# A two-layer mLSTM, attention and RG-LRU backbone: the attention's second projection group as steps between the attention units

## The chip, the cores and the metric

The kernel runs on one core of a Trainium2 chip, in one launch. The metric is the device time of the launch in microseconds; a figure for a kernel is the median of several runs.

## What is computed

Two layers work on 1024 latent tokens (a grid of 16 rows and 64 columns) and 256 context tokens of width 1024, all in f32. Of each layer the part in question is the neighbourhood attention of 8 heads of 64: projections q, k, v from the normed input, an RMS norm of q and k, scores against a window of 8 x 16 grid places with a relative bias and against all 256 context tokens, softmax, and the weighted sum of v.

```python
def row_block(r):
    sr = jnp.clip(r - wr // 2, 0, rows - wr)
    q_r = lax.dynamic_index_in_dim(qg, r, axis=1, keepdims=False)
    k_band = lax.dynamic_slice_in_dim(kg, sr, wr, axis=1)
    ...
    s_loc = jnp.einsum('bqhd,brqchd->bhqrc', q_r, k_win).astype(jnp.float32) * scale
    dr = sr + jnp.arange(wr) - r + (WIN_R_MAX - 1)
    bias = jnp.transpose(rpb[:, dr][:, :, dc], (0, 2, 1, 3))
    s_loc = (s_loc + bias.astype(jnp.float32)).reshape(b_, NA_HEADS, GRID_W, wr * wc)
    s_ctx = jnp.einsum('bqhd,bkhd->bhqk', q_r, kc).astype(jnp.float32) * scale
    p = jax.nn.softmax(jnp.concatenate([s_loc, s_ctx], axis=-1), axis=-1).astype(v.dtype)
```

Beside it in each layer run an mLSTM of 4 heads, an RG-LRU, the output projection over all three, and an MLP of hidden width 4096. Context tokens attend to context alone, and have no output in the second layer.

## The kernel before

**Split matmuls.** Every f32 weight and activation is split into a rounded high part and a low rest (`wh`, `wl` by `load_w`; `xh`, `xlo`), and each product takes three matmuls: high-high, high-low, low-high. An input projection of one token tile (128 tokens, 256 columns) is 24 matmuls into one PSUM bank (`proj_tm`).

**PSUM.** Eight banks: one `p`, one `q`, three `a`, two `b`, one `c`. `bank("pq")` takes turns between p and q.

**Stages of a layer.** RG-LRU and mLSTM projections; the mLSTM's state and output (`ml_state`, `ml_out`); then attention. The eight heads are two groups of four, and each group two pairs. `na_group(grp)` projects k, q and v of a group (10 token tiles each in layer 0; q only 8 in layer 1), ScalarE copies each result (`uev`), squares it for the norm (`usq`), and the copy goes to DRAM (`u_nk`, `u_nq`, `u_nv`). Group 0 stands in the program right behind `ml_out`, group 1 behind group 0.

**Preparation.** `na_prep(hp)` makes the stacks of a pair of heads: it loads `ut`, multiplies by the norm, transposes on TensorE, and writes split keys and queries (`KH`, `KL`, `QS`), of which one partition half is filled by DMAs from the other half. There are two sets of stacks, for even and for odd pairs. Pair 0 is prepared before attention begins; pair hp + 1 is prepared in six (layer 1: five) parts beside the units of pair hp.

**Attention units.** `na_att(hp)` has 10 units a pair in layer 0 (two of context queries, eight of latent ones) and 8 in layer 1, so 40 and 32. A unit computes scores into the three `a` banks (L834, L838; context L780), VectorE adds the table and takes the maximum (L848, L852), ScalarE takes the exponential, `side()` issues other work, and `softmax_pv` transposes (L727), scales and multiplies by v (L757).

**Tables.** The relative bias of a head is expanded by DMAs on GpSimd's queue from `R_d` to `E_d` to `T_d` in DRAM (`tab_expand`, `tab_rows`). Each pair loads three sets of two tables (`tab`, four buffers), and GpSimd adds to each a combined mask (`crm`, rows and columns, six made per program).

**The filler.** `side()` also issues `fill()`, the first half of the output projection (L1363, bank p, evacuated by VectorE at L1380 with `xs`), 24 steps over 40 units in layer 0, 16 over 32 in layer 1.

**Modulation.** In layer 0, `mod_pairs` loads 32 blocks of `w_mod` in 16 pairs (`mr`, two buffers) and multiplies them (L316), one pair at every third projection step of both groups.

**Order.** The program is recorded in the order of the code, and a list scheduler with a time model then arranges each engine's instructions. So the order of the code sets priorities; what stands in each engine's queue is what the scheduler made of it. Nearly all DMAs go through SP's queue, in order.

## Time and profile before

| what | before |
|---|---|
| median of 3 runs | 3124.81 us (3122.93 to 3128.83) |
| profiled execution | 3124.27 us, span 3122.5 us |
| TensorE busy | 3020.2 us, 97% |
| VectorE busy | 1900.0 us, 61% |
| ScalarE busy | 1128.4 us, 36% |
| GpSimd busy | 291.0 us, 9% |
| mean granted TensorE clock | 0.988 |
| attention, layer 0 | about 510 to 755 us |
| attention, layer 1 | about 2125 to 2347 us |

TensorE's busy share counts a matmul from issue to end, and matmuls overlap, so "busy" is not "at its peak". The granted clock of a stretch is the mean over its time at two levels, 1.2 and 2.4 GHz: 1.00 is all at 2.4. The attention stages are found by their first scores and last products with v.

### The profile page before, as it was taken

The numbers are of one execution on the slowest core, as the hardware profiler recorded it, in microseconds if no ns is written. First come the engines' busy times: TensorE is split into PE (matmuls) and PEld (weight loads), VectorE is DVE, ScalarE is ACT, GpSimd is POOL, SyncE is SP. The second block draws the span as 40 slices with busy tenths as digits, with TensorE's granted clock in tenths as the row PEclk, the third lists the DMA queues.
The fourth block names the chain that finished last, engine by engine and source line by source line (L and its number), as shares of the span: only waits on it lengthen the run. The fifth ranks groups of instructions, "written<-read, shape, count | busy, mean of one in ns | idle before, by whom it ended". The sixth has DMA issues, their size and how long they took to land.

```text
span 3122.5 us, 47474 instructions
## 1 busy us (share of the span) xinstructions
PE 3020.2 (97%) x18250; PEld 2558.1 (82%) x18250; DVE 1900.0 (61%) x4318; ACT 1128.4 (36%) x2011; POOL 291.0 (9%) x252
## 2 busy tenths in 40 slices
PE   7999998999899999999999999998899999999999
PEld 6888898778788888887778889997787777887877
DVE  5757655787977667455444574765787444444444
ACT  4632223574421222233222453234564222332222
POOL 0410000222200000010000511002222000000000
PEclk8999999999999999999999999999999999999999
DMA  9624567765233444233323632347753332333233
GB/s 272 216 73 144 171 190 199 226 169 178 68 115 105 126 124 125 75 108 101 95 88 94 175 123 82 100 131 219 219 172 110 95 95 89 99 116 91 92 96 93
DMA packets 531098, 410.73 MB, mean 132 GB/s; under 512 B 27580, under 2 KB 496536, under 8 KB 530872
## 3 DMA queue, kind: packets, MB, share of 16 engines
q1 hardware_dynamic: 519448, 387.41, 41.9%
q0 software_dynamic: 8576, 15.00, 1.5%
q10 hardware_dynamic: 2848, 5.28, 0.5%
q8 instruction: 144, 2.36, 0.3%
q14 instruction: 82, 0.67, 0.1%
HBM read 339.72 MB, written 67.53 MB: 130 GB/s over the span
## 4 chain that ended last, share of the span: by engine, by line
PE 70%; DVE 11%; DMA 10%; issue 2%; ACT 2%; SPq 1%; POOL 0%; ACTq 0%; DVEq 0%; POOLq 0%
PE psa L468 14%; PE psa L1515 13%; PE psq L468 5%; PE psp L468 5%; PE psp L1515 4%; DMA mr<-in_w_mod_dram 4%; PE psq L1515 4%; PE psp L483 4%; PE psq L483 3%; PE psp L1363 3%; DVE ma L344 3%; PE psc L757 2%; PE psb L727 1%; PE psa L1363 1%; PE psa L834 1%
## 5 line engine op out<-in xcount | busy, mean ns | idle before, releaser
L200 ACT ACTIVATE wh<-wr 128x1024 fp32r<-128x1024 f32 (+3 forms) x356 | 361.8, 1021 | 929.7 <-PE psa L1515 296.3
L201 DVE TENSOR_TENSOR wl<-wr,wh 128x1024 fp32r<-128x1024 f32 (+3 forms) x356 | 424.5, 1196 | 380.6 <-ACT wh L200 374.3
L468 PE MATMUL psa<-xlo,wh 128*128 128x512 f32 (+1 forms) x856 | 319.5, 373 | 2.2 <-DVE xlo L444 2.1
L468 PE MATMUL psa<-xh,wh 128*128 128x512 f32 (+1 forms) x856 | 318.8, 373 | 2.4 <-ACT xh L443 2.4
L468 PE MATMUL psa<-xh,wl 128*128 128x512 f32 (+1 forms) x856 | 319.3, 373 | 1.4 <-DVE wl L201 1.4
L1515 PE MATMUL psa<-hl,wh 128*128 128x512 f32 (+1 forms) x768 | 286.1, 373 | 1.3 <-DVE hl L211 1.3
L1515 PE MATMUL psa<-hh,wh 128*128 128x512 f32 (+1 forms) x768 | 284.6, 376 | 0.6 <-ACT wh L200 0.5
L1515 PE MATMUL psa<-hh,wl 128*128 128x512 f32 (+1 forms) x768 | 278.1, 373 | 0.6 <-DVE wl L201 0.6
L1519 DVE SCALAR_TENSOR_TENSOR res<-psa,modt,res 128x512 f32<-128x512 f32 (+1 forms) x192 | 130.9, 693 | 165.8 <-PE psa L1515 165.6
L468 PEld LDWEIGHTS psa<-xlo,wh 128*128 128x128 f32 x856 | 161.6, 189 | 33.4 <-DVE xlo L444 2.9
L468 PEld LDWEIGHTS psa<-xh,wh 128*128 128x128 f32 x856 | 161.5, 189 | 33.4 <-ACT xh L443 2.8
L468 PEld LDWEIGHTS psa<-xh,wl 128*128 128x128 f32 x856 | 161.6, 189 | 32.5 <-DVE wl L201 2.2
L409 POOL TENSOR_TENSOR acc<-acc,nsq 128x512 f32<-128x512 f32 (+1 forms) x56 | 80.3, 1446 | 1020.6 <-ACT nsq L408 970.7
L210 ACT ACTIVATE hh<-rl 128x512 fp32r<-128x512 f32 (+1 forms) x160 | 93.5, 589 | 225.0 <-DVE rl L1491 225.0
L1515 PEld LDWEIGHTS psa<-hh,wh 128*128 128x128 f32 x768 | 144.5, 188 | 34.8 <-ACT wh L200 8.9
L483 PE MATMUL psp<-wl,xh 128*128 128x256 f32 (+1 forms) x560 | 163.1, 291 | 5.9 <-DVE wl L201 5.8
L1515 PEld LDWEIGHTS psa<-hh,wl 128*128 128x128 f32 x768 | 144.5, 188 | 28.6 <-DVE wl L201 1.5
L1515 PEld LDWEIGHTS psa<-hl,wh 128*128 128x128 f32 x768 | 144.6, 188 | 27.8 <-DVE hl L211 1.5
L483 PE MATMUL psp<-wh,xh 128*128 128x256 f32 (+1 forms) x560 | 162.2, 290 | 2.5 <-ACT wh L200 2.4
L483 PE MATMUL psq<-wh,xh 128*128 128x256 f32 (+1 forms) x560 | 162.7, 290 | 1.4 <-ACT usq L641 0.8
L483 PE MATMUL psq<-wl,xh 128*128 128x256 f32 (+1 forms) x560 | 160.9, 287 | 0.0
L483 PE MATMUL psq<-wh,xlo 128*128 128x256 f32 (+1 forms) x560 | 160.2, 286 | 0.0
(409 smaller groups left out, 7342.4 us busy)
## 6 DMA issues: line engine op xcount, KB each, us to landing
wr<-in_w_mlp_dram SPq DMA_DIRECT2D x256, 512.0 KB
mr<-in_w_mod_dram SPq DMA_DIRECT2D x92, 512.0 KB
wr<-in_w_in_dram SPq DMA_DIRECT2D x48, 512.0 KB
tab<-T_d SPq DMA_DIRECT2D x48, 384.0 KB
T_d<-E_d POOLq DMA_DIRECT2D x48, 256.0 KB, 6.5
ab<-row_d SPq DMA_DIRECT2D x36, 256.0 KB
xT_d<-res SPq DMA_DIRECT2D x4, 2048.0 KB
wr<-in_w_out_dram SPq DMA_DIRECT2D x32, 256.0 KB
```

Of the source, the lines that this page charges most:

```text
L200: act.activation(hi[:, a:b], raw[:, a:b], AF.Copy)
L201: dve.tensor_sub(lo[:, a:b], raw[:, a:b], hi[:, a:b].bitcast(F32))
L210: act.activation(hi, src32, AF.Copy)
L344: dve.scalar_tensor_tensor(a, raw[:, k], s[:, k], a, op0=OP.mult, op1=OP.add)
L409: pool.tensor_add(acc[bi], acc[bi], sq[:, :n])
L468: m = pe.matmul(t[:, :n], w[a][:, k, :], X[bi][b][:, k, :], start=(i == 0), stop=(i == 23))
L483: m = pe.matmul(t[:, :cols], X[bi][b][:, half * 4 + k, o:o + P], ws[half][a][:, k, :], start=(i == 0), stop=(i == 23))
L727: pe.transpose(t[:w, j * P:(j + 1) * P], S[e][:, o:o + w], permT)
L757: pe.matmul(to[64 * e:64 * e + 64, :P], vals[i][:w, 64 * e:64 * e + 64], PT[:w, e, i], start=(i == 0), stop=(i == nt - 1))
L1363: pe.matmul(t[:, :n], w[a][:, k, cc * P:(cc + 1) * P], Y[bi][b][:, k], start=(i == 0), stop=(i == 11))
L1515: m = pe.matmul(t[:, :n], w[a][:, k, cc * P:(cc + 1) * P], H[bi, k][b], start=(i == 0), stop=(i == 3 * GH - 1))
L1519: dve.scalar_tensor_tensor(xr[bi][:, ct], t[:, :n], G2[:, ct, v:v + 1], xr[bi][:, ct], op0=OP.mult, op1=OP.add)
```

## The change

- **Group 1's projections become steps.** `proj_tm` yields after each token tile. `proj = na_group(1, "p")` uses bank p alone. Five steps stand beside the preparation of pair 0 and five beside that of pair 1; the other 20 (layer 1: 18) are spread over the first 15 (12) attention units. The norms of q and k come before v.
- **The filler is moved behind them.** The output projection's first half now spreads over the remaining 25 (20) units, and its pools are opened when the last projection step is done.
- **One set of stacks.** Pairs 0, 1 and 3 write the same buffers, pair 2 others. Pair 1 is prepared after pair 0's units, no longer beside them; pairs 2 and 3 still beside units.
- **Column masks in the bias.** `tab_mask` loads each third of `E_d`, adds the column mask on GpSimd and stores it, before `tab_rows`. In the units GpSimd adds the row mask alone, with a broadcast operand; `crm` is gone. `tab` has three buffers.
- **Modulation.** Layer 0's pairs of loads advance at four of every seven steps of group 0, and all are done before group 1.

```diff
+    def tab_mask(l, ct, et):
+        ed = E_d[l][:, ct]
+        pool.dma_start(et, ed)
+        pool.tensor_add(et, et, colm[:, ct, None, :].to_broadcast([P, 23, 32]))
+        pool.dma_start(ed, et)
...
-                if mcount[0] % 3 == 0:
+                if mcount[0] * 4 % 7 < 4:
                     next(mods[0], None)
-            proj_tm(ws, 256, X, toks, ev)
+            for tt in toks:
+                proj_tm(ws, 256, X, [tt], ev, banks)
+                yield
...
-                    tb_ = npl.tile([P, 2, 384], F32, name=nm("tab"), tag="tab", bufs=4)
+                    tb_ = npl.tile([P, 2, 384], F32, name=nm("tab"), tag="tab", bufs=3)
...
-                    pool.tensor_add(tv, tv, crm[ct].rearrange("p (r c) -> p r c", c=32))
+                    pool.tensor_add(tv, tv, masks[:, 96:120].unsqueeze(2).to_broadcast([P, 24, 32]))
...
+        spools = {0: ns, 1: ns, 3: ns}
+        preps = [na_prep(hp, ns, spools, stk[hp]) for hp in range(4)]
+        proj = na_group(1, "p")
...
+        def open_late():
+            run(proj)
+            close_x()
+            for n_ in ("yk", "nt", "yh"):
+                g_ = tc.tile_pool(name=f"{n_}_{l}", bufs=1, side=sides[0], reuse_waits="tile")
+                late[n_] = (g_, g_.__enter__())
+            spools[2] = late["nt"][1]
...
+            n_hp = 8 if last else 10
+            n_side = 4 * n_hp
+            n_proj = n_hp + n_hp // 2
+            def prep_beside(hp):
+                for i, _ in enumerate(preps[hp]):
+                    if i < 5:
+                        next(proj, None)
...
             for hp in range(4):
                 def side():
+                    u = pace["at"]
+                    pace["at"] += 1
+                    if u < n_proj:
+                        for _ in range(due("proj", u, n_proj)):
+                            next(proj, None)
+                        if u == n_proj - 1:
+                            open_late()
+                        return
-                        for _ in range(1):
-                            next(preps[hp + 1], None)
-                    for _ in range(due("fill")):
+                    if 1 <= hp < 3:
+                        next(preps[hp + 1], None)
+                    for _ in range(due("fill", u - n_proj, n_side - n_proj)):
```

TensorE's queue where attention begins in layer 0, before (L692 is transposes of a preparation, L483 projections, L780 the context scores, L1363 the filler):

```order
L483 MATMUL psq_5680<-wh_5423,xlo_794 128x256
L692 MATMUL psb_5800<-idj,ut_5797 128x2x4x16 x2
L692 MATMUL psb_5815<-idj,ut_5812 128x2x4x16 x4
L780 MATMUL psa_5851<-KH_5742,QS_5740 128x256
...
L780 MATMUL psa_5903<-KL_5745,QS_5741 128x256
L1363 MATMUL psp_5976<-yh_5933,wh_5970 128x256
```

The same place after (L707 and L705 are the transposes, L793 the context scores; each run of L483 is shown by its first row):

```order
L707 MATMUL psb_4936<-idj,ut_4933 128x128 x2
L483 MATMUL psp_5241<-wh_4799,xh_793 128x256
...
L705 MATMUL psb_4980<-idj,ut_4977 128x2x4x16 x4
L483 MATMUL psp_5241<-wh_4807,xlo_794 128x256
...
L793 MATMUL psa_5041<-KH_4784,QS_4782 128x256
...
L483 MATMUL psp_5334<-wh_4799,xh_793 128x256
...
L793 MATMUL psa_5041<-KH_4785,QS_4783 128x256
```

Steps of group 1, all in bank p, stand around the first scores where the filler followed them.

TensorE's queue between pair 0's last products with v (L757) and pair 1's first scores (L780) in layer 0, before:

```order
L753 MATMUL psc_6436<-idj,rb_6434 128x128
L757 MATMUL psc_6436<-PT_6412,VB_6366 64x128 x6
...
L727 MATMUL psq_6568<-idj,S_6531 128x128 x2
...
L838 MATMUL psa_6605<-KL_5745,QS_5741 128x256
L780 MATMUL psa_6685<-KH_5871,QS_5869 128x256
```

And after (L766 and L770 end a unit of pair 0, L707 and L705 are pair 1's preparation, L793 its first scores):

```order
L766 MATMUL psc_6034<-idj,rb_6032 128x128
L770 MATMUL psc_6034<-PT_6014,VB_5830 64x128 x6
...
L707 MATMUL psq_6059<-idj,ut_6056 128x128 x2
L707 MATMUL psb_6100<-idj,ut_6097 128x128 x4
L483 MATMUL psp_6066<-wh_5435,xh_793 128x256
...
L707 MATMUL psb_6143<-idj,ut_6140 128x128 x4
...
L705 MATMUL psb_6274<-idj,ut_6271 128x2x4x16 x4
L483 MATMUL psp_6202<-wh_6189,xh_261 128x256
...
L793 MATMUL psa_6332<-KH_6052,QS_6050 128x256
```

Pair 1's whole preparation, with steps between its parts, now stands between the pairs.

SP's queue around the tables of pair 0 in layer 0, before (`tab` loads of the second set are 6188 and 6191, for its first and second head):

```order
L808 DMA tab_6011<-T_d_96 128x2x384
L808 DMA tab_6014<-T_d_96 128x2x384
...
L808 DMA tab_6188<-T_d_96 128x2x384
L708 DMA QS_5741<-ql_5805 64x512
L708 DMA QS_5741<-ql_5820 64x512
L808 DMA tab_6191<-T_d_96 128x2x384
L817 DMA VB_6194<-u_nv_82 32x4x128 x2
```

And after (the second head's table of the second set is 5402; behind it the third set's first, then projections' stores):

```order
L721 DMA QS_4783<-ql_5031 64x512
L645 DMA u_nq_78<-uev_5566 128x256
L821 DMA tab_5402<-T_d_96 128x2x384
L821 DMA tab_5824<-T_d_96 128x2x384
L645 DMA u_nq_78<-uev_5597 128x256
L645 DMA u_nq_78<-uev_5691 128x256
L830 DMA VB_5830<-u_nv_82 32x4x128 x4
```

The second head's load has moved behind the stacks' copies and stands between stores of the projections.

## Rows read from the trace of the kernel before

**Rows 1.** The page, part 1: busy us, share of the span, instructions.

```profile
PE 3020.2 (97%) x18250; PEld 2558.1 (82%) x18250; DVE 1900.0 (61%) x4318; ACT 1128.4 (36%) x2011; POOL 291.0 (9%) x252
```

**Rows 2.** Stretches: length; busy us of PE, PEld, DVE, ACT, POOL; clock; DMA share; GB/s.

```profile
245.00:440.00 195.00, 186.94 (x1733) 172.20 (x1732) 136.47 (x510) 47.06 (x108) 7.80 (x6) 0.98 0.57 162
...
510.00:575.00 65.00, 55.31 (x374) 46.25 (x373) 46.48 (x126) 32.85 (x76) 11.71 (x6) 0.89 0.83 233
575.00:690.00 115.00, 103.87 (x888) 88.35 (x888) 97.26 (x313) 75.34 (x201) 27.52 (x15) 0.97 0.71 195
690.00:755.00 65.00, 65.00 (x551) 55.78 (x549) 41.62 (x142) 34.47 (x93) 6.20 (x4) 1.00 0.50 166
...
2120.00:2190.00 70.00, 59.07 (x392) 48.97 (x391) 47.45 (x112) 34.11 (x74) 22.18 (x12) 0.95 0.90 251
2190.00:2310.00 120.00, 109.18 (x907) 89.11 (x906) 98.19 (x310) 72.99 (x188) 31.06 (x17) 0.97 0.70 205
```

**Rows 3.** TensorE's waits, 510 to 575 us: who for whom, total us, times, longest.

```profile
PE psp L1363 <- DVE xs L1380: 4.9, 2, 2.7
...
PE psp L1363 <- ACT wh L200: 1.3, 1, 1.3
PE psp L1363 <- DVE wl L201: 0.8, 1, 0.8
```

**Rows 4.** Timeline of TensorE, filler: start us, duration us, instruction.

```profile
520.52 1.06 PE L1363 MATMUL psp<-yh,wh 128*128 128x512 f32 x2
...
533.89 0.63 PE L1363 MATMUL psp<-yh,wh 128*128 128x512 f32 x2
```

**Rows 5.** The same, first matmuls of two projection steps in a row.

```profile
500.99 0.28 PE L483 MATMUL psq<-wh,xh 128*128 128x256 f32 x1
...
503.84 0.28 PE L483 MATMUL psp<-wh,xh 128*128 128x256 f32 x1
```

**Rows 6.** Timeline of ScalarE: copy and square of one projection step.

```profile
480.82 0.38 ACT L637 ACTIVATE uev<-psq 128x256 f32<-128x256 f32 x1 [0.27 <-PE psq L483]
481.10 0.38 ACT L641 ACTIVATE usq<-psq 128x256 f32<-128x256 f32 x1
```

**Rows 7.** Groups by line: busy us, mean ns; idle before. VectorE in the preparations.

```profile
L684 DVE TENSOR_TENSOR ut<-ut,rsn 128x512 f32<-128x512 f32 (+1 forms) x44 | 30.7, 699 | 46.7 <-DMA ut<-u_nk 34.3 <-DMA ut<-u_nq 12.0
...
L701 DVE TENSOR_TENSOR KL<-psb,KH 64x512 fp32r<-64x512 f32 (+1 forms) x36 | 21.5, 596 | 2.2 <-ACT KH L700 1.7
```

**Rows 8.** The same for GpSimd's additions.

```profile
L811 POOL TENSOR_TENSOR tab<-tab,crm 128x768 f32<-128x768 f32 x48 | 91.0, 1910 | 354.2 <-DMA tab<-T_d 266.9 <-DVE m L852 29.2 <-DVE yr L866 22.8
...
L1409 POOL TENSOR_TENSOR crm<-crm,masks 128x768 f32<-128x768 f32 x6 | 11.2, 1896 | 0.0
```

**Rows 9.** Timeline of GpSimd in layer 1: last table DMAs, first rotary product.

```profile
1798.95 3.51 POOL L611 DMA_DIRECT2D T_d<-E_d  x6 [0.99 <-issue]
1837.12 2.70 POOL L1079 TENSOR_TENSOR kT<-rraw,rope 128x512 f32<-128x512 f32 x1 [34.66 <-ACT rraw L1076]
```

**Rows 10.** Timelines of GpSimd and of SP: table loads, and additions.

```profile
612.97 1.83 POOL L811 TENSOR_TENSOR tab<-tab,crm 128x768 f32<-128x768 f32 x1 [24.16 <-DMA tab<-T_d]
...
637.06 3.62 POOL L811 TENSOR_TENSOR tab<-tab,crm 128x768 f32<-128x768 f32 x2 [19.99 <-DMA tab<-T_d]
...
605.49 0.88 SPq L808 DMA_DIRECT2D tab<-T_d  x1
...
633.79 0.93 SPq L808 DMA_DIRECT2D tab<-T_d  x2
```

**Rows 11.** VectorE by line and form, 510 to 755 us: one instruction a unit.

```profile
L751 DVE COPY rb<-den 128x128 f32<-128x128 f32 x40 | 15.1, 378 | 2.6 <-PE psc L753 2.1
```

**Rows 12.** Modulation: instructions of mr; timelines of SP and TensorE, one pair.

```profile
L316 PE MATMUL psc<-mr,cact x512: 269/273/423, 258.0 to 474.2; 128*32 128x128 f32 x171
...
326.23 1.32 SPq L305 DMA_DIRECT2D mr<-in_w_mod_dram  x2
...
335.49 1.08 PE L316 MATMUL psc<-mr,cact 128*32 128x128 f32 x32 [0.21 <-DMA mr<-in_w_mod_dram]
```

More of the change, by code (lines that the diff above doesn't have):

```diff
@@ L629, in backbone_kernel, with na_proj @@
         mcount = [0]
[L631 removed]
+        def na_proj(grp, c0, dst, toks, stat, banks="pq"):
             ws = [load_w(win[l, h_ * 512:(h_ + 1) * 512, c0 + grp * 256:c0 + grp * 256 + 256]
@@ L662, in na_group, with na_prep @@
                 rsn[kd, grp] = y
-        def na_prep(hp, npl, stacks):
+        def na_prep(hp, npl, pools, stacks):
             grp = hp // 2
             h0 = (hp % 2) * 2
-            QS = [npl.tile([P, NTOK], F32R, name=nm("QS"), tag="QS%d" % (hp % 2), bufs=2) for _ in range(2)]
-            KH = [npl.tile([P, NTOK], F32R, name=nm("KH"), tag="KH%d" % (hp % 2), bufs=2) for _ in range(2)]
-            KL = [npl.tile([P, NTOK], F32R, name=nm("KL"), tag="KL%d" % (hp % 2), bufs=2) for _ in range(2)]
+            QS, KH, KL = ([pools[hp].tile([P, NTOK], F32R, name=nm(n_), tag=n_, bufs=2) for _ in range(2)]
+                          for n_ in ("QS", "KH", "KL"))
             stacks += [QS, KH, KL]
@@ L1015, in backbone_kernel @@
                 tab_expand(l)
+                for ct in range(3):
+                    tab_mask(l, ct, lp.tile([P, 23, 32], F32, name=nm("et"), tag="et"))
                 qT = [m1.tile([P, NTOK], F32, name=f"qT{l}{p_}", tag=f"qT{p_}") for p_ in range(2)]
@@ L1386, in fill @@
                     phase(f"oproj{l}")
+                    yp = late["yh"][1]
                     Yh = {bi: [yp.tile([P, 4, BLKS[bi][1]], F32R, name=nm("yh"), tag=f"yh{min(bi, 1)}{j}")
@@ L1421, in side @@
                             next(filler, None)
-                    phase(f"mod{l}")
-                    tick(due("mod"))
-                    pace["at"] += 1
+                phase(f"na_prep{l}")
+                if hp < 2:
+                    prep_beside(hp)
                 phase(f"na_att{l}")
-                yr = yk.tile([P, NTOK], F32, name=nm("yr"), tag="yr")
+                yr = npl.tile([P, NTOK], F32, name=nm("yr"), tag="yr") if hp < 2 else \
+                    late["yk"][1].tile([P, NTOK], F32, name=nm("yr"), tag="yr")
                 na_att(hp, npl, stk[hp], yr, side)
-                if 0 <= hp < 3:
+                if 1 <= hp < 3:
                     run(preps[hp + 1])
@@ L1432, in backbone_kernel @@
                 pass
-            tick(64)
-        ns_cm.__exit__(None, None, None)
+        yk_cm, yk = late["yk"]
+        for g_ in (late["yh"][0], late["nt"][0], na_cm, ns_cm):
+            g_.__exit__(None, None, None)
         phase(f"oproj{l}")
```

54 lines of the change are left out of this document (20 added, 34 removed).

## The prediction

> **What bounds the kernel now.** I read the page's busy shares first: TensorE is busy 97% of the span and no other engine over 61% [rows 1]. So time can only come out of stretches in which TensorE is not full, and I looked for those in the table of stretches [rows 2]. In each row there, the stretch less "PE busy" is idle time, and the stretch times (1 - granted clock) is what the half clock costs, because a clock of 0.89 means that 22% of the stretch ran at 1.2 GHz and gave half its work. For the two attention stages:
>
> - layer 0, 510 to 575 us: 9.7 idle, 7.2 clock; 575 to 690: 11.1 and 3.5; 690 to 755: nothing
> - layer 1, 2120 to 2190: 10.9 and 3.5; 2190 to 2310: 10.8 and 3.6
>
> That is 31.3 us in the two opening stretches and 29.0 in the two middle ones, together 60.3 us or 1.9% of the span. It is all that a better order of the same matmuls can win in these stages; the change takes no matmul away. Next I asked what ends those waits. In the opening stretches it is the start of the filler, the first half of the output projection: its matmuls (L1363) wait for their evacuation and for their weights, and the evacuation for its DMA [rows 3]. What the half clock does is to be seen in one and the same triple of matmuls: two of them take 1.06 us behind the wait and 0.63 us later [rows 4]. In the middle stretches VectorE is busy 85% and 82%, against 64% in the last one, where TensorE is full [rows 2].
>
> **The change, part by part.** The sum is made against the profiled execution, 3124.27 us (span 3122.5 and 1.8 around it); the median of the three runs shown is 0.5 us more.
>
> *Second group's projections between the units.* 30 steps (28 in layer 1) of 24 matmuls move from a stretch of their own to a place beside the preparations of pairs 0 and 1 and the first 15 (12) attention units. A step is 2.85 us [rows 5], so 85 and 80 us of work that depends on nothing in the attention fill the opening. The filler's own start is moved behind them. So the 31.3 us of the opening stretches go: **-31.3**.
>
> *One bank in place of two.* The steps now use bank p alone. A step can begin only when ScalarE has emptied the bank: copy and square took 0.66 us from start to end [rows 6], with the tail of the last matmul (0.28 us long, pitch 0.12 [rows 5]) and the signals about 0.9 us. Where attention matmuls stand between two steps this is hidden. In the changed order 13 steps of layer 0 and 16 of layer 1 follow the one before with less than 0.9 us of other matmuls between, most of them in the two preparations. Counting what stands there, 7 and 9 us stay open: **+16**. Bounds: 5 (ScalarE ready earlier, transposes fill) and 27 (all 29 bare, 0.9 each).
>
> *The filler starts later.* Its 24 (16) steps now share 25 (20) units in place of 40 (32). Its first evacuations and weights still come late; 7.0 us of such waits in layer 0's opening [rows 3], about as much in layer 1. Now attention matmuls stand around them; I take 3 each: **+6**, bounds 0 and 14.
>
> *The middle.* Per unit, TensorE has 0.96 filler steps (0.8 in layer 1) in place of 0.6 (0.5), and VectorE has their evacuation and weight splits too. VectorE at 85% gives little room, so I leave two thirds of the 29.0 us standing: **-10**. Bounds: -29 (all covered) and +15 (VectorE becomes the bound and the loss grows by half).
>
> *One set of stacks.* Pair 1's KH, KL and QS are written over pair 0's, so its preparation waits for pair 0's last scores. In the order two units' softmax matmuls and four and a half steps, some 18 us, stand between those scores and pair 1's first. The chain in between (three K segments, a copy between partition halves, the first Q segment) I put at 12 us: six segments with one multiplication of 0.70 and two subtractions of 0.60 are 11.4 us of VectorE [rows 7], part of it ahead of pair 0's last scores, and a copy's landing. Cover exceeds chain: 0, and up to +8 a layer if the cover is gone.
>
> *Masks.* The 48 additions on GpSimd stay, 1.91 us each; one operand is now a broadcast of the row mask, and the addition that already had such an operand took 1.90 [rows 8]. The six tables crm go. Six loads, additions and stores come in front of the expansion of the tables, on GpSimd's queue. In layer 1 the queue is done at 1802.5 and the next work on it, the rotary product that TensorE's state stage needs, starts at 1837.1 [rows 9]; 35 us of slack hide three times a load, 1.9 us and a store. 0, bounds 0 and +10.
>
> *Three table buffers in place of four.* The second head's table of each set now takes the buffer of the set before, first head, and can be loaded only after that head's last unit. From the issue to the addition 3.3 to 7.5 us passed [rows 10], and 1.9 us for the addition: 5.2 to 9.4. The next unit asks for it one unit later; a unit took 245/40 = 6.1 us [rows 11]. What waits behind that load on SP's queue are stores of the projections. I take 0.3 us at each of 22 boundaries: **+6**, bounds 0 and 70.
>
> *Modulation in the first group.* The 16 pairs of loads of layer 0 spread over 258 to 474 us before, 13.5 us a pair, and now have to pass by about 440, 11.4 a pair. A pair that was waited for took 9.3 us from issue to matmul, and its matmuls 1.1 [rows 12]; the stretch has a DMA share of 0.57 [rows 2]. It fits barely: **+2**, bounds 0 and 40.
>
> Sum: -31.3 + 16 + 6 - 10 + 6 + 2 = -11.3, so 3124.3 - 11.3 = **3113 us**.
>
> **The rivals.**
>
> *R1, everything is won.* The middle stretches are filled too (-29 in place of -10) and half the handovers are covered: 3113 - 19 - 8 = 3086. For it: in 690 to 755, with filler and no preparation, nothing is lost [rows 2]. Against it: VectorE's share in the middle.
>
> *R2, the gain is given back.* VectorE binds in the units that now carry filler and a preparation, and the middle loses what the opening won: 3113 + 10 = 3123, no change.
>
> *R3, the tables come late; this one ends slower.* If the path of a table is 7.6 us, near its mean of 7.3, and nothing else hides it, each of the 22 boundaries stops VectorE 1.5 us, which holds three banks and with them TensorE: 33 in place of 6, 3140. It decides from 1.1 us per boundary. For it: 7.5 us did occur, and more transfers now stand in the same queue. Against it: the projection units are longer than 6.1 us, with one and a third steps each.
>
> *R4, the modulation loads bind.* With the loads closer together a pair may need 1.25 times 9.3 and 1.1, 12.7 us, 1.3 more than there is: 16 x 1.3 = 21, 3134.
>
> *R5, the handovers drop the clock.* After a gap of 2.72 us TensorE ran at 1.2 GHz for a whole filler step [rows 3, 4]. If 0.9 us did the same, every bare handover would cost a step at half clock, 2.85 us: 29 x 2.85 = 83, 3196. Against it: from 245 to 440 us TensorE idles 8 us in short pieces and the clock is granted at 0.98 [rows 2]. The Trainium skill, TensorE: Matmul & The Clock Gate, section "A second HAM failure mode: psum-queue depth-cycling", tells of a kernel whose banks took turns so that small gaps between groups of matmuls made the clock oscillate; by that rule this change would be slower by R5's price, and this row of the trace doesn't bear it out.
>
> **How the numbers follow.** Differences under 0.2% (6.2 us) can't be told from no change here. Chances: the forecast 0.39, R1 0.12, R2 0.23, R3 0.17, R4 0.06, R5 0.03. Faster is the forecast and R1, 0.51; same is R2, 0.23; slower the rest, 0.26. The range takes in R1 with 4 us to spare, and R4 and R3 with 6: 3082 to 3146. Outside lie R5, the long end of R3 and a piece of R1. The forecast's own range is 3100 to 3118.
>
> **What would show it.** In the profile after, the opening of each attention stage should have a granted clock of 1.00 and no wait of L1376 there; TensorE's waits for ScalarE's copy and square should add up to some 16 us (the handovers); the middle of the stage, with pairs 2 and 3, should show the remaining clock below 1.00 and VectorE above 80%. A wait of VectorE or TensorE for the table's addition speaks for R3, a wait of L316 for its DMA for R4, a clock below 0.95 in the projection units for R5. The forecast is wrong if TensorE's idle time from 440 us to the end of layer 0's attention is not smaller than before, or if the two layers differ: all terms but the modulation's are in both.

## The result and the profile after

The changed kernel takes **3180.0 us** (median of 4 runs, 3176.4 to 3183.3) against 3126.6 for the kernel before (4 runs beside it): a ratio of 1.0172, 95% interval 1.0154 to 1.0189, so 53 us slower. Forecast were 3113. The profiled execution took 3180.0, with a span of 3178.2.

Part 1 of its page, to be held against [rows 1]: the matmuls are the same in number and the other engines' work nearly so (GpSimd's fell by 25 us), and TensorE's share fell from 97% to 95%.

```profile
PE 3034.2 (95%) x18250; PEld 2572.6 (81%) x18250; DVE 1904.4 (60%) x4318; ACT 1133.6 (36%) x2011; POOL 266.3 (8%) x258
```

To see where, I cut both spans at the same events: first matmul of a layer's state stage, last one of the output stage's transposes (ysb), first one of the MLP's second product (L1515, now L1546). Both output stages hold the projections of group 0, and some of group 1. Lengths in us; the rows below that of after are experiments. Ratios are to the kernel before, run on the same chip as the experiment, where its median was 3129.6 to 3137.7; before_again is its trace on one of those chips. Edits that left a stage alone moved it by up to 5 us (a_nomask, layer 0's output stage), a_prep's by 9 (194.0 in that stage), and layer 1's attention is 7 us longer in before_again than in the first trace, so a smaller difference between two single traces says nothing.

| kernel | to state L0 | output L0 | attention L0 | MLP L0, to state L1 | output L1 | attention L1 | MLP L1 | ratio |
|---|---|---|---|---|---|---|---|---|
| before | 258.4 | 175.1 | 415.4 | 1090.1 | 149.5 | 322.4 | 704.9 | 1 |
| before_again | 258.2 | 176.1 | 417.7 | 1090.8 | 149.9 | 329.4 | 704.9 | 1 |
| **after** | 264.5 | 185.2 | 441.0 | 1088.1 | 145.2 | 343.9 | 703.7 | 1.0172 |
| b_bank | 258.4 | 176.1 | 449.8 | 1089.9 | 145.1 | 358.0 | 704.9 | 1.0174 |
| b_masks | 267.6 | 175.2 | 422.8 | 1091.1 | 152.9 | 339.8 | 704.8 | 1.0061 |
| b_mods | 259.9 | 190.5 | 419.1 | 1087.4 | 150.8 | 324.9 | 704.8 | 1.0014 |
| b_sq | 258.8 | 174.5 | 418.0 | 1093.2 | 150.4 | 326.6 | 703.8 | 0.9991 |
| a_nomask | 258.2 | 190.3 | 441.6 | 1092.3 | 145.2 | 345.1 | 703.6 | 1.0153 |
| a_pq | 264.5 | 185.7 | 445.2 | 1089.7 | 147.0 | 365.4 | 703.7 | 1.0248 |
| a_sq | 262.0 | 183.1 | 429.9 | 1090.7 | 145.9 | 336.9 | 704.1 | 1.0106 |
| a_nproj | 266.6 | 187.3 | 421.3 | 1086.9 | 147.2 | 343.6 | 704.8 | 1.0096 |
| a_nproj5 | 265.3 | 185.4 | 432.1 | 1089.1 | 147.3 | 347.4 | 703.7 | 1.0140 |
| a_npmd | 265.2 | 174.7 | 444.2 | 1089.0 | 148.8 | 343.5 | 704.6 | 1.0141 |
| a_npsqhalf | 266.7 | 184.7 | 419.5 | 1088.5 | 146.2 | 339.0 | 703.7 | 1.0086 |
| a3_nomask | 258.4 | 187.2 | 419.0 | 1097.1 | 144.9 | 334.9 | 704.9 | 1.0087 |

Of the 55.7 us that the span grew, 6 stand before layer 0's state stage, 10 in its output stage, 26 and 22 in the two attention stages; layer 1's output stage is 4 shorter, because fewer of the second group's matmuls are done in it (742 matmuls of projections in place of 843). Next the stretches of after (columns as in [rows 2]).

```profile
264.50:449.70 185.20, 166.03 (x1658) 152.39 (x1656) 126.95 (x465) 38.24 (x82) 0.00 (x0) 0.96 0.61 175
449.70:500.00 50.30, 39.71 (x269) 37.20 (x268) 24.36 (x57) 20.24 (x51) 4.40 (x3) 0.86 0.65 174
500.00:607.90 107.90, 103.47 (x944) 97.05 (x943) 62.11 (x225) 56.65 (x151) 11.82 (x8) 0.98 0.41 119
607.90:680.00 72.10, 58.15 (x418) 47.67 (x417) 55.17 (x154) 41.41 (x98) 8.90 (x6) 0.91 0.89 233
680.00:781.60 101.60, 97.17 (x754) 82.94 (x753) 63.77 (x202) 49.99 (x128) 10.38 (x7) 0.97 0.61 190
781.60:848.50 66.90, 59.25 (x299) 49.50 (x297) 49.99 (x108) 26.88 (x46) 22.77 (x19) 0.95 0.41 127
2124.00:2165.00 41.00, 30.11 (x198) 27.84 (x197) 15.94 (x35) 12.46 (x30) 4.40 (x3) 0.88 0.73 195
2165.00:2247.10 82.10, 78.07 (x712) 72.41 (x711) 52.66 (x192) 45.29 (x118) 11.93 (x8) 0.98 0.47 136
2247.10:2401.60 154.50, 141.11 (x1052) 114.64 (x1050) 111.45 (x324) 84.87 (x202) 19.26 (x13) 0.98 0.78 224
```

The steps stand in 449.7 to 607.9 (26 of 30) and 2124 to 2247 (17 of 28); the others stand in the output stages. Where they run between the units (500 to 607.9, 2165 to 2247) little is lost, as I had hoped: 4.4 idle in 108 us, 4.0 in 82. But each stage now opens twice. At 449.7 and 2124 pair 0's preparation runs with five steps beside it, idle 10.6 and 10.9 us and the clock at 0.86 and 0.88. At 607.9 the filler starts: idle 14.0, clock 0.91, DMA share 0.89. TensorE's waits (columns as in [rows 3]) in these two places, 440 to 612 and 607 to 680 us:

```profile
PE psp L483 <- ACT usq L648: 5.4, 7, 1.7
PE psb L707 <- DVE ut L697: 4.6, 2, 3.2
PE psa L793 <- issue: 2.9, 1, 2.9
PE psb L705 <- DVE rsn L168: 1.3, 1, 1.3
...
PE psa L793 <- DMA QS<-ql: 3.0, 2, 2.0
PE psp L1376 <- DVE xs L1400: 2.8, 2, 2.6
PE psp L1376 <- ACT yh L210: 2.5, 1, 2.5
```

The first row is the handover of bank p. The second, the fourth and the first of the second place are links of a preparation's chain; for the third the profile names no cause. The last two are the filler's first evacuations and the splits of its input. Behind the last unit of layer 0 TensorE also waits 7.0 us for the second half's input (xh, L210), which before was split beside the last units.

### The profile page after: what moved, and what is told of

Same layout as the page of the kernel before. It is cut to its first block, busy times and chain, and to the rows that moved or that the text cites. A ratio compares the mean times of both kernels' runs of the same rounds, so it can differ in the third digit from the quotient of the medians.

```text
span 3178.2 us, 47469 instructions
## 1 busy us (share of the span) xinstructions
PE 3034.2 (95%) x18250; PEld 2572.6 (81%) x18250; DVE 1904.4 (60%) x4318; ACT 1133.6 (36%) x2011; POOL 266.3 (8%) x258
## 4 chain that ended last, share of the span: by engine, by line
PE 73%; DMA 9%; DVE 9%; ACT 3%; issue 2%; SPq 1%; ACTq 0%; DVEq 0%
PE psa L468 15%; PE psa L1546 14%; PE psp L483 6%; PE psq L468 5%; PE psp L468 5%; PE psp L1546 5%; PE psq L1546 5%; DMA mr<-in_w_mod_dram 4%; PE psp L1376 3%; PE psc L770 2%; PE psq L483 2%; DVE ma L344 2%; PE psa L1376 2%; PE psb L740 1%; PE psa L847 1%
## 5 line engine op out<-in xcount | busy, mean ns | idle before, releaser
L1546 PE MATMUL psa<-hl,wh 128*128 128x512 f32 (+1 forms) x768 | 286.0, 372 | 1.5 <-DVE hl L211 1.5
L1546 PE MATMUL psa<-hh,wh 128*128 128x512 f32 (+1 forms) x768 | 284.4, 375 | 0.4 <-ACT wh L200 0.3
L1546 PE MATMUL psa<-hh,wl 128*128 128x512 f32 (+1 forms) x768 | 278.1, 373 | 0.7 <-DVE wl L201 0.7
L483 PE MATMUL psp<-wh,xh 128*128 128x256 f32 (+1 forms) x792 | 236.5, 299 | 15.6 <-ACT usq L648 12.6
L483 PE MATMUL psp<-wl,xh 128*128 128x256 f32 (+1 forms) x792 | 233.1, 294 | 4.9 <-DVE wl L201 4.7
L483 PE MATMUL psp<-wh,xlo 128*128 128x256 f32 (+1 forms) x792 | 229.4, 290 | 0.0
L483 PEld LDWEIGHTS psp<-wh,xh 128*128 128x128 f32 x792 | 156.1, 197 | 23.2 <-ACT usq L648 17.5
L1546 PEld LDWEIGHTS psa<-hh,wh 128*128 128x128 f32 x768 | 144.3, 188 | 34.9 <-ACT wh L200 8.9
L210 ACT ACTIVATE hh<-rl 128x512 fp32r<-128x512 f32 (+1 forms) x160 | 93.5, 589 | 210.2 <-DVE rl L1522 210.2
L1546 PEld LDWEIGHTS psa<-hh,wl 128*128 128x128 f32 x768 | 144.3, 188 | 28.8 <-DVE wl L201 1.5
L1546 PEld LDWEIGHTS psa<-hl,wh 128*128 128x128 f32 x768 | 144.4, 188 | 28.5 <-DVE hl L211 1.7
L483 PEld LDWEIGHTS psp<-wl,xh 128*128 128x128 f32 x792 | 156.0, 197 | 8.4 <-DVE wl L201 6.2
```

Source lines behind the costliest of these rows:

```text
L210: act.activation(hi, src32, AF.Copy)
L483: m = pe.matmul(t[:, :cols], X[bi][b][:, half * 4 + k, o:o + P], ws[half][a][:, k, :], start=(i == 0), stop=(i == 23))
L1546: m = pe.matmul(t[:, :n], w[a][:, k, cc * P:(cc + 1) * P], H[bi, k][b], start=(i == 0), stop=(i == 3 * GH - 1))
```

## The experiments

### One part alone, in the kernel before

**b_bank.** The second group's steps on one bank, nothing moved in the program.

```diff
+            banks = "p" if grp else "pq"
...
-            proj_tm(ws, 256, X, toks, ev)
+            for tt in toks:
+                proj_tm(ws, 256, X, [tt], ev, banks)
```

> The kernel before, with the second group's 58 steps on bank p alone, where they stood. It measures a handover by itself. Theory A (a bare handover is a short wait): 0.4 to 0.9 us at each step that has no other matmuls behind it, 20 to 50 us in all, 3147 to 3177, with the granted clock of these stretches at 0.97 or more. Theory B (handovers drop the clock): a step at half clock for each, some 2.85 us on top, over 3250, with the clock below 0.8 in the stretch from 433 to 510 us. Theory C (the steps of this stretch interleave with the preparation and hide it): under 10 us, 3135.

Measured: 3192.1 against 3137.7, ratio 1.0174 (1.0157 to 1.0192), 54.5 us, as much as the whole change and just above Theory A's upper end. But the steps did not stay where they stood: with the single bank the planner chose another order. First the row of layer 0's opening stretch in the kernel before, then its steps and context scores from 433.5 us on (count, ns, first and last start), then the same steps and scores of b_bank:

```profile
433.50:510.00 76.50, 75.45 (x727) 74.01 (x726) 27.47 (x74) 24.65 (x61) 4.96 (x3) 1.00 0.67 188
...
L483 PE MATMUL psq<-wh,xh x96: 274/281/385, 435.8 to 509.4; 128*128 128x256 f32 x96
...
L780 PE MATMUL psa<-KH,QS x16: 278/283/366, 510.3 to 688.7; 128*128 128x256 f32 x16
...
L483 PE MATMUL psp<-wh,xh x192: 274/282/582, 435.3 to 545.5; 128*128 128x256 f32 x192
...
L782 PE MATMUL psa<-KH,QS x16: 279/282/365, 472.3 to 722.6; 128*128 128x256 f32 x16
```

Before, all the steps left for this place, 24 of the 30, end ahead of the first scores at 510.3. In b_bank 7 do, and 17 stand between the units, as in the changed kernel (5 and 21). So the run prices one bank together with the order that follows from it, not a handover by itself, and 0.94 us, its loss over the 58 steps, is no handover's price. The stretch of pair 0's preparation lost 1 us (433.5 to 510, all of it idle) and now loses 18; its row, and the waits from 425 to 560:

```profile
434.50:520.00 85.50, 72.16 (x630) 66.48 (x631) 33.00 (x83) 24.30 (x57) 5.25 (x3) 0.94 0.60 157
...
PE psp L483 <- ACT usq L642: 8.4, 10, 1.2
PE psp L483 <- ACT uev L638: 8.1, 9, 3.1
```

That is 19 waits of 0.87 us in the mean; with 15.4 us of the same waits in layer 1 (1974 to 2200 us), 32 of the 54.5 us are waits for the bank. The clock fell to 0.94, not below 0.8, so a handover is not a step at half clock. The Trainium skill (TensorE: Matmul & The Clock Gate, section "A second HAM failure mode: psum-queue depth-cycling") has such small gaps make the clock oscillate; in this stretch the granted clock fell from 1.00 to 0.94, which costs 5 us in 85.5, far from R5's 2.85 for each handover.

**b_masks.** Only the masks, as in the change (added to E_d in DRAM, crm gone).

> The kernel before, with the masks of the change alone: the column mask is added to the expanded tables in DRAM (three loads, additions and stores on GpSimd's queue in each layer) and the addition in the unit has the row mask as a broadcast; the six tables crm are gone. Theory A (GpSimd's chain): in the changed kernel layer 0's state stage begins 6.1 us later (264.5 against 258.4) while layer 1's stretch before its state stage keeps its length (208.9 against 208.5), so the masks alone cost about 6 us, all of it before layer 0's state stage: some 3132. Theory B (the prediction's term, and the 6 us belong to another part of the change): 0, 3127, and layer 0's state stage begins at 258.

Measured: 3156.6, 1.0061 (1.0041 to 1.0081), 19 us: more than either theory. State L0 begins at 267.6, later as Theory A has it, by 9 us where it said 6. The other 10 us stand in layer 1's attention (339.8 against 329.4), where GpSimd's addition is faster than before (1.48 us in place of 1.83) and nobody waits for it. What differs there is the order in which the planner put the attention's instructions. I count these 10 us as the order's, without having shown it: in b_sq the order there differs too, and the stage takes 326.6.

**b_mods.** Only the modulation's pace.

```diff
-                if mcount[0] % 3 == 0:
+                if mcount[0] * 4 % 7 < 4:
...
                 na_group(0)
+                run(mods[0])
```

> The kernel before, with the pace of the modulation alone: four of seven evacuations ask for a pair of loads in place of one of three, and all are asked for by the end of the first group. Theory A (the loads bind): TensorE's waits for them rise from 1.0 us to about the 11.4 us of the changed kernel, the stage of layer 0's output and first group becomes 10 us longer as there (185.2 against 175.1), and the second group's stretch, which loses its loads, gives back 1 to 5: 3132 to 3136. Theory B (the prediction's +2; the stage grew for another reason): 3127 to 3129. Layer 1 has no such loads, so by both it keeps its length.

Measured: 3142.9, 1.0014 (1.0002 to 1.0026), 4 us. The stage grew by 14 (190.5), with 8.6 us of waits for the loads in place of 1.2, so the loads bind there. The timed runs show 4 of these 14 at the end; the profiled execution was one of the longer ones (3145.8) and doesn't show where the rest comes back. The stage's row and the wait, 260 to 450 us:

```profile
259.90:450.40 190.50, 173.81 (x1688) 160.87 (x1686) 129.26 (x468) 38.76 (x84) 1.34 (x2) 0.93 0.63 171
...
PE psc L316 <- DMA mr<-in_w_mod_dram: 8.6, 5, 3.0
```

**before_again.** The kernel before, for its trace.

> The kernel before, unchanged, on the chip of these runs, for its trace stage by stage: the same times as the rows shown, or where this chip differs. By both theories of the other runs the ratio is 1.000.

Measured: 3135.6, beside 3135.5 in the same runs.

### One part undone, in the changed kernel

**a_pq.** Both banks for the second group again (`proj = na_group(1)`).

> The changed kernel with the second group's steps on the two banks p and q by turns, as before. Theory A (the one bank is the main cost; in b_bank it cost 54.5 us for 58 steps, 0.94 a step, and here at least the 29 steps that the prediction counted are bare, at most all 58): 27 to 54 us come back, a ratio to the kernel before of 1.000 to 1.009. Theory B (the prediction's term, most of it hidden by the attention's matmuls): 16 us, 1.012. Theory C (bank q is wanted by the transposes of the softmax and of the preparations, so the steps wait there instead): 1.017 or more.

Measured: 3213.0, 1.0248 (1.0224 to 1.0271): 24 us slower still, Theory C. Waits in layer 1, 2027 to 2260 us, where after has 4.3 in place of the first and none of the others:

```profile
PE psb L707 <- DVE ut L697: 13.9, 4, 7.9
...
PE psb L705 <- DVE KL L714: 4.7, 1, 4.7
PE psq L483 <- DVE KL L714: 1.9, 1, 1.9
```

The preparation's transposes take banks b, b and q by turns from pair 1 on, and a step that wants q now stands behind VectorE's splits, and they behind it. So this run doesn't give the one bank's price in the new place; it shows that the second bank is no longer free there.

**a_sq.** The square reads the copy, so that the bank is free 0.3 us sooner.

```diff
-                    act.activation(sq, t, AF.Square)
+                    act.activation(sq, u if grp else t, AF.Square)
```

> The changed kernel with the square of the second group's K and Q steps taken from the copy in SBUF in place of the bank, so that ScalarE gives bank p back after the copy alone (some 0.3 us sooner at 40 of 58 steps); the work is the same. Theory A (handovers cost what the trace shows, 12.6 us of waits for the square and the half clock behind them, some 16): a third to a half of that, 5 to 8 us, comes back, 1.015. Theory B (every one of the 58 handovers is bare, as in b_bank, 54 us): 12 us or more, 1.013 or less. Theory C (handovers are hidden): 1.017.

Measured: 3169.3, 1.0106 (1.0080 to 1.0132): some 21 us back, beyond Theory A. The first steps of layer 0's opening in after and in a_sq (start, duration, instruction; in brackets idle time before and who ended it):

```profile
451.72 0.58 PE L483 MATMUL psp<-wh,xh 128*128 128x256 f32 x1 [1.72 <-ACT usq L648]
457.07 0.39 PE L483 MATMUL psp<-wh,xh 128*128 128x256 f32 x1 [0.75 <-ACT usq L648]
467.65 0.63 PE L707 MATMUL psb<-idj,ut 128*128 128x128 f32 x4 [3.17 <-DVE ut L697]
```

```profile
445.62 0.39 PE L483 MATMUL psp<-wh,xh 128*128 128x256 f32 x1 [0.26 <-ACT uev L644]
449.21 0.38 PE L483 MATMUL psp<-wh,xh 128*128 128x256 f32 x1 [0.47 <-ACT uev L644]
452.79 0.39 PE L483 MATMUL psp<-wh,xh 128*128 128x256 f32 x1 [0.47 <-ACT uev L644]
463.48 0.84 PE L707 MATMUL psb<-idj,ut 128*128 128x128 f32 x4 [4.00 <-DVE ut L697]
```

And the opening of a_sq as a stretch:

```profile
445.10:495.00 49.90, 40.52 (x317) 38.31 (x316) 25.40 (x66) 24.40 (x61) 4.86 (x4) 0.97 0.71 188
```

Idle time fell only from 10.6 to 9.4, since the preparation's own waits stayed (4.00 and others); the clock rose from 0.86 to 0.97, which is 5.5 us. In after a matmul of a step took 0.58 behind the wait of 1.72, and 0.39 behind that of 0.75. Over both layers the waits of the steps fell from 14.2 to 8.8 us. These 5.4, the 5.5 of the clock here, and about 3 of the clock in layer 1 make up two thirds of the 21; the rest I can't place. The planner's order differs here too (layer 0 has 6 steps ahead of the first scores and 20 behind, after 5 and 21), and the profiled execution was the shortest of the four, 8 us under their median; so how much of the 21 is the shorter hold alone is not shown.

**b_sq.** The same edit in the kernel before.

> The kernel before with the square of the second group's K and Q steps taken from the copy in SBUF. With two banks a step has the next step's 2.85 us to hand its bank back, so by Theory A (a_sq's gain is the shorter handover) nothing changes, 0.999 to 1.001. Theory B (reading SBUF in place of the bank helps ScalarE, or the order falls better): 5 us or more, 0.998 or less.

Measured: 3133.2, 0.9991 (0.9977 to 1.0004): no difference. With two banks a shorter hold wins nothing, so a_sq's gain is no gain of the square itself.

**a_half.** Two steps share a buffer, one half each.

```diff
+    held = []
...
-            t = bank(banks)
+            if banks != "p":
+                t = bank(banks)
+            elif held:
+                t = held.pop()
+            else:
+                t = bank(banks)
+                held.append(t[:, 256:])
```

> The changed kernel with bank p cut into two halves for the second group: two steps that follow each other write columns 0 to 255 and 256 to 511 of one buffer (a step needs 256 of its 512), so only every second step waits for ScalarE. Theory A (the bare handovers are the largest cost, 0.94 us for each of the 58 steps in b_bank): 20 to 27 us come back, 1.008 to 1.011. Theory B (they cost the 12.6 us that the trace shows as waits, and a_sq's gain was for the most part another order): 6 to 8 us, 1.015.

Measured: 3183.6, 1.0167 (1.0139 to 1.0195). It tells neither theory apart, because the waits are still there: two steps in a row both wait for the square before them, so the program's dependency holds for the whole buffer. TensorE's matmuls stand in the same order as in after in both attention stages.

```profile
451.19 0.39 PE L491 MATMUL psp<-wh,xh 128*128 128x256 f32 x1 [1.51 <-ACT usq L656]
455.85 0.39 PE L491 MATMUL psp<-wh,xh 128*128 128x256 f32 x1 [1.54 <-ACT usq L656]
```

**a_nomask.** Masks as before.

> The changed kernel with the masks as before: no column mask added in DRAM, and six tables crm, here of 16-bit floats to fit, added in the unit. Theory A (what the masks cost in the kernel before, 1.0061, they cost here): 1.011. Theory B (in b_masks most of it came from another order of the attention's work, not from the masks; here only what stands before layer 0's state stage comes back, 6 us): 1.015. Theory C (nothing): 1.017.

Measured: 3183.6, 1.0153 (1.0134 to 1.0172); the interval touches after's, so Theory B and no effect can't be told apart by the time. By the trace state L0 begins at 258.2 again, so the 6 us at the front are the masks', but layer 0's output stage is 5 longer and the stretch before state L1 is not shorter (211.5 against 208.9). Its first stretch, and that before state L1:

```profile
0.00:258.20 258.20, 238.23 (x1623) 203.91 (x1623) 160.81 (x362) 120.88 (x191) 50.44 (x70) 0.97 0.61 182
...
1770.90:1982.40 211.50, 202.95 (x1216) 176.46 (x1215) 122.82 (x201) 89.12 (x136) 60.96 (x74) 0.98 0.43 129
```

**a_pqnomask.** Both undone.

> The changed kernel with both undone: banks p and q by turns, masks as before. What is left of the change is the move of the steps, the shared stacks, three table buffers and the modulation's pace. Theory A (both costs are whole, 54 and 19): 0.994, and the move itself is then a gain of some 20 us. Theory B (half the handovers, 27, and 6 for the masks): 1.007, the move loses as well. Between them 1.000.

Measured: 3214.2, 1.0241 (1.0218 to 1.0263), the same as a_pq and outside both theories. Bank q is shared here as in a_pq; I take that to be the reason.

**a_prep.** More cover for pair 0's preparation.

```diff
-            pace = {"fill": sum(8 * len(p_) for p_ in parts), "proj": 20 + len(QT) - 10, "at": 0}
+            pace = {"fill": sum(8 * len(p_) for p_ in parts), "proj": 20 + len(QT) - 15, "at": 0}
...
-                    if i < 5:
+                    for _ in range((2 - hp) * (i < 5)):
                         next(proj, None)
```

> The changed kernel with two projection steps in place of one beside each of the first five steps of pair 0's preparation (ten there in place of five, and five fewer between the units). Theory A (pair 0's preparation lost its cover: in the kernel before all 30 steps could stand beside it and its stretch loses 1 us, in the changed kernel 449.7 to 500 us loses 10.6 us idle and some 6 by the clock): more cover brings back 6 to 10 us a layer, 3160 to 3168. Theory B (the loss there is the handover of bank p): two steps in a row add handovers, 3180 to 3186.

Measured: 3195.6, 1.0187 (1.0160 to 1.0213), the direction of Theory B. But it tests neither, because the planner did not put ten steps there: layer 0 has 5 steps ahead of the first scores and 21 behind, exactly as after, and the same waits (1.39, 1.56 and 0.59 us for the square, 3.81 for ut). Projection steps alone in the 50.3 us behind the output stage, in after and in a_prep (columns as in [rows 2], of TensorE only):

```profile
449.70:500.00 50.30, 32.86 (x210) 30.78 (x210) 0.86 0.65 174
...
459.60:509.90 50.30, 30.39 (x204) 28.54 (x203) 0.90 0.67 176
```

So whether more cover would shorten that stretch stays open.

**a_nproj and a_nproj5.** The steps in the first 10 (8) units, or in the first 5 (4; `n_hp // 2`), and the filler from there on.

```diff
-            n_proj = n_hp + n_hp // 2
+            n_proj = n_hp
```

> The changed kernel with the steps between the units spread over the first 10 (8) units in place of 15 (12), so that the first half of the output projection begins a third earlier and has 30 (24) units. Theory A (the late filler is what lengthens the end of layer 0's attention: 73 more matmuls and 4.6 us more idle behind the last unit than before, 17.8 us): about half of that comes back, 1.014, and fewer of the output projection's matmuls stand behind the last unit. Theory B (two steps a unit in place of one and a third are two bare handovers more often): 15 to 20 us more, 1.022.

> The changed kernel with the steps between the units in the first 5 (4) units, four a unit; the output projection's first half then has 35 (28) units. Going from 15 (12) to 10 (8) units gave 24 us. Theory A (the later the filler starts, the more it lacks at the end and the denser its transfers are): another step of the same kind, 5 to 12 us less than 3167 on that chip, 1.006 to 1.008. Theory B (a place for the steps in pair 0's units is enough, and four bare steps in a row bring more handovers): equal or slower, 1.010 to 1.014.

Measured: a_nproj 3167.2, 1.0096 (1.0080 to 1.0113), 24 us better than after; a_nproj5 3178.8, 1.0140 (1.0120 to 1.0159). In a_nproj what the trace shows of it is in layer 0's attention (421.3 against 441.0), none in layer 1's. Theory A has the direction but not the place: all 288 matmuls of the output projection's second half still stand behind the last unit (after 288, before 217). What vanished is the second opening: the 72 us at the filler's start in a_nproj, to be read against 607.9 to 680 of after, and the densest 20 us of after:

```profile
603.30:675.40 72.10, 65.96 (x522) 55.81 (x520) 57.12 (x172) 42.66 (x105) 8.89 (x6) 0.95 0.78 221
...
620.00:640.00 20.00, 13.61 (x95) 10.89 (x94) 13.83 (x41) 11.34 (x27) 2.96 (x2) 0.77 1.04 257
```

It is idle 6.1 us, not 14.0. In after, side() takes neither a step of pair 2's preparation nor of the filler before unit 15, so both begin there: Y's loads, its weights, the loads of u and the copies of K between the halves come in one burst. From unit 10 on, pair 2's preparation has ten units in place of five. The filler's own start hardly moves; what moves is that preparation. Four traces side by side, with the loss (idle and half clock) from 600 to 640 us:

| kernel | pair 2's transposes | filler's first matmul | lost, 600 to 640 us |
|---|---|---|---|
| after | 594 to 638 us | 612 us | 15 us |
| a_nproj5 | 583 to 620 us | 598 us | 15 us |
| a_nproj | 577 to 608 us | 607 us | 5 us |
| a_npsqhalf | 571 to 602 us | 602 us | 5 us |

Where the preparation is done, or nearly, when the filler begins, 5 us are lost; where they overlap, 15.

**a_npmd.** a_nproj with the modulation spread as before, its pool held open through the steps (and two buffers VB in place of three).

> The kernel a_nproj with the modulation as before: one pair of loads asked for by every third step, running on beside the second group's steps until these end (the pool of its tiles stays open until then; two buffers of values in place of three make the room). Theory A (the pace makes layer 0's output stage lose 15 to 18 us more than before): that stage returns to about 131 us from 142, and of it 5 to 12 us arrive at the end, 1.006 to 1.008. Theory B (b_mods' 1.0014 is all there is; the loads then run into the attention's own): 1.008 to 1.010. Layer 1 keeps its length.

Measured: 3179.3, 1.0141 (1.0118 to 1.0164), 14 us slower than a_nproj. The output stage went back to its old length, as Theory A has it, but the attention stage grew by more:

```profile
265.20:439.90 174.70, 164.47 (x1557) 150.15 (x1554) 124.97 (x459) 40.07 (x88) 0.00 (x0) 1.00 0.59 163
439.90:780.60 340.70, 299.78 (x2480) 263.54 (x2479) 208.16 (x644) 165.89 (x420) 36.92 (x24) 0.94 0.67 188
```

Whether the loads, the third VB or the modulation's matmuls do that was not separated.

### Together

**a_npsq and a_npsqhalf.** a_nproj's and a_sq's edits; the second with a_half's too.

> The changed kernel with the steps in the first 10 (8) units and the square taken from the copy: the two single edits that gave 24 and 21 us. Theory A (the filler's late start and the handovers are two costs): 45 us together, 1.003. Theory B (both work by shortening the same stretch of pair 0 and 1, or by a luckier order): no more than the better of the two, 1.009 to 1.011.

> The changed kernel with all three: the steps in the first 10 (8) units, the square taken from the copy, bank p in two halves. Theory A (handovers are the largest cost and the filler's start the next): 0.996 to 1.001, no slower than the kernel before. Theory B (one cost, or order): 1.006 to 1.010. What no part of it touches are the masks' 6 us and the modulation's 4.

Measured: 3163.1, 1.0097 (1.0074 to 1.0120), and 3156.8, 1.0086 (1.0057 to 1.0116). Theory B: the gains of 24 and 21 don't add up. In a_npsqhalf the steps' waits are down to 0.26, 0.47 and 0.47 us in the opening, and layer 0's attention takes 419.5 us, as long as in before_again (417.7). So with both costs gone the move neither wins nor loses there; layer 1's attention is still 10 us longer (339.0 against 329.4).

**a3_nomask and a3_prep.** a_npsqhalf with the masks as before, or with a_prep's edit.

> The kernel a_npsqhalf with the masks as before (six tables crm, of 16-bit floats). Theory A (the masks cost GpSimd's chain in front of layer 0's state stage, as a_nomask showed with 258.2 in place of 264.5): 6 to 8 us come back, 1.006, and the state stage begins at 258. Theory B (the whole 19 us of b_masks): 1.002. The rest against the kernel before, 18 us by Theory A, is then layer 0's output stage with the modulation (9 us) and layer 1's stage of output and first group (5 us idle more).

> The kernel a_npsqhalf with two projection steps beside each of the first five steps of pair 0's preparation. Theory A (pair 0's preparation lacks matmuls beside it, since the handovers that spoiled a_prep are halved here): the 11 us lost in layer 0 between 451 and 500 us fall to 5, as much in layer 1, some 10 us less, 1.005. Theory B (the waits of the preparation follow from its own chain, a load of K rows, two multiplications, transposes, splits and a copy, and the matmuls put beside it come in the wrong place): no gain, 1.008 to 1.012.

Measured: a3_nomask 3156.0, 1.0087 (1.0071 to 1.0103): no gain, neither theory. The 8 us at the front came back (258.4), but the stretch before state L1 grew by as much (MLP and this stretch 1097.1 against 1088.5); its row:

```profile
1746.20:1961.70 215.50, 206.85 (x1216) 180.39 (x1215) 123.22 (x203) 88.97 (x136) 60.70 (x74) 0.97 0.42 126
```

So undoing the masks here wins nothing clear of the noise, where alone in the kernel before they cost 19 us; what makes layer 1 longer without them I don't know. a3_prep 3165.2, 1.0114 (1.0098 to 1.0130), in Theory B's range, but it tests no more than a_prep did: layer 0 has 6 steps ahead of the first scores with and without the edit. None of these versions reaches the kernel before.

## Why the prediction was wrong

The sign was wrong. I compare lost time, idle and half clock, as the prediction did; the first four points make 57 us, of which 2 to 4 come back in the MLPs and in front of layer 1's state stage: 53 to 55 of the 55.7. This says where the time is lost; the experiments say only in part why.

- **Steps between the units, -31.3, and handovers, +16: together -15.3; measured +18.** This is the step that failed. The units with steps do run full, but the loss of the openings did not go, because I priced the place to which the steps go and not the one that they leave. Before, 24 of the 30 steps stood ahead of the first scores, beside pair 0's preparation, and lost 1 us in 76; left there are five, on one bank, and 449.7 to 500 us lose 17.6. Counted over both parts (433.5 to 575 before, 449.7 to 607.9 after) layer 0's opening lost 17.9 and loses 24.2, layer 1's lost 15.5 and loses 21.5, and 5 us more are lost in its output stage. The handovers were sized well as waits (14.2 us; 0.87 each in layer 0 of b_bank, 0.9 predicted). That more is lost than these waits is shown by b_bank, which loses 54 us with 32 of such waits, and by a_sq, which wins back 21 with 5.4 fewer; both also have another order, and how much each part does was not separated. That the missing cover is what makes the preparation's stretch slow is argued, not shown: neither a_prep nor a3_prep put more steps there.
- **Filler later, +6, and middle, -10: together -4; measured +18** (13 and 2 in the units of the two layers, 3 behind the last units). In layer 0 the filler's start lost 20.4 us in 72, and the four traces set side by side under a_nproj lose that much only where its start falls together with pair 2's preparation. I had seen that it moves, and counted its 7 us of first waits; not that the early return in side() starts two chains and their transfers in one unit. VectorE, R2's suspect, was busy 77% there and 63% later, against 85% in the middle before, which speaks against it as the bound.
- **Modulation, +2 (0 to 40): measured +15 in its stage,** and R4's mechanism: waits for mr of 11.4 us from 265 to 460 us. All runs of the table with the old pace take 174.5 to 176.1 us there, those with the new one 183.1 to 190.5. In the kernel before the whole program paid only 4 for the same stage (b_mods); undone in a_nproj it made the attention stage longer by more (a_npmd). So the stage's cost is shown, its share in the 53 us isn't.
- **Masks, 0: measured +6 before layer 0's state stage.** Runs of the table with the old masks reach that stage at 258.2 to 259.9 us, those with the new ones at 262.0 to 267.6. I looked for slack in layer 1 and found 35 us; layer 0's queue I didn't look at. TensorE's matmuls up to there stand in the same order as before. Two of its waits for VectorE grew: one for cv at 145 us, where before had none, to 2.0 us, and one for a weight split from 0.95 to 4.1 us (after, then before):

```profile
192.75 0.58 PE L483 MATMUL psp<-wl,xh 128*128 128x256 f32 x1 [4.09 <-DVE wl L201]
...
188.00 0.39 PE L483 MATMUL psp<-wl,xh 128*128 128x256 f32 x1 [0.95 <-DVE wl L201]
```

How the additions and table DMAs of the masks, which stand on GpSimd's queue from 103 to 180 us, delay VectorE is not shown. In all the masks cost 19 us alone (b_masks); undone in the changed kernels they gave nothing clear of the noise (a_nomask, a3_nomask).

- **Tables, +6 and R3:** VectorE waited for the addition 0.9 us in layer 0 and 3.8 in layer 1 (rows below, 450 to 782 and 2124 to 2402 us), TensorE never; so by the waits three buffers were enough. Four were not tried.

```profile
DVE S L861 <- POOL tab L824: 0.9, 1, 0.9
...
DVE S L861 <- POOL tab L824: 3.8, 4, 1.8
```

- **One set of stacks, 0:** not tried, since a second set finds no room in the changed layout. Pair 1's preparation shows some 4 us of waits in each layer, no more than a preparation's chain shows elsewhere.
- **R5, the handovers drop the clock,** gave 3196 and came nearest, but not by its mechanism: a wait is not always followed by a slow matmul (0.39 us behind 1.51 and 1.54 in a_half, 0.58 behind 1.72 in after), the clock in the units with steps was 0.98, and b_bank's whole loss, 0.94 us a step, is a third of the 2.85 that R5 puts on the clock alone. That its number is near is luck.

Of the signs that I had named against the forecast, the plain one came: from 440 us to the end of layer 0's attention TensorE's idle time rose from 21.9 to 34.2 us. The layers differ in what a_nproj mends (20 us of layer 0's attention, none of layer 1's); that they grew by 26 and 22 us is within the noise of one trace. Open remain how the loss divides between the one bank and the order that comes with it, a third of a_sq's gain, why it doesn't add to a_nproj's, and how much of b_masks' time is order alone.

## What to carry to other kernels

Work that is moved to fill idle time may be hiding something where it stands: put a price on the stretch that it leaves before counting on the one that it enters. When a double buffer is cut to a single one for a move, measure that cut alone first; here that one run lost as much as the whole change. Where a planner arranges the instructions, look in the trace whether an edit did what it was made for: b_bank moved the steps without being told to, and a_prep, told to move them, did not. And where a new order starts two chains at one point, stagger them.

## What the runs showed of the hardware

I had not expected that a wait's cost shows elsewhere: shortening the hold of a bank by about 0.3 us at 40 steps removed 5.4 us of waits but some 21 us of time, in part by the granted clock of one stretch, 0.86 to 0.97, in part perhaps by the order that changed with it. And GpSimd's addition with the row mask, one value repeated along each row of 32, took 1.48 us (median of 48) against 1.83 with a full table of the same size. The addition from which I had taken 1.90 repeats a whole row of 32 values, and its median was 1.84, as slow as the full table's.
